# Hybrid decoder layer, one core: an opening on raw x with two gate tiles, and a merge with its gate halves in place

## The chip, the cores and the metric

The kernel runs on one NeuronCore of a Trainium2 chip. The metric is device time in microseconds (us); before the change the median of three runs is 1577.41 us (1577.34 to 1582.8). The engines are PE (TensorE: products), DVE (VectorE), ACT (ScalarE), POOL (GpSimd) and SP (which only issues DMAs). Each takes its instructions in order; they wait for one another by semaphores.

## The reference, cut to what matters

One decoder layer, sequence 1024, width 1024, all float32, x transposed to (channel, time) by the host.

```python
h = rms_norm(x, norm_mix_pre)
proj = h @ w_in        # [RWKV r,k,v, decay, rate, gate downs | S5 input u | two gates of 1024]
gates = sigmoid(proj[..., N_RWKV_COLS + S5_WIDTH:] + b_gate)
o_rwkv = rwkv7_branch(p_rwkv, ...) @ w_branch_rwkv       # a delta-rule state over time, 8 heads
o_s5   = s5_branch(u_s5, ...) @ w_branch_s5              # scan, GELU, sigmoid GLU
mixed  = (g_rwkv * o_rwkv + g_s5 * o_s5) @ w_out
x = x + rms_norm(mixed, norm_mix_post)
f = conv_ffn(rms_norm(x, norm_ffn_pre), ...)             # gated, width-3 convolution
x = x + rms_norm(f, norm_ffn_post)
```

The norm is `x * rsqrt(mean(x*x)) * g`: one factor per time step and one per channel. The factor per time step commutes with a product over channels.

## The kernel before, in words

Each float32 product is three products of halves: both operands are split into a high part (rounded, by ACT) and the rest (by DVE), and PE sums high*high, high*rest and rest*high (L174, L175, L176). One k-step is such a triple for 128 channels; a tile of output is 128 x 512 over eight k-steps. Time is cut into two halves of 512. Weights come by `load_w` (L156 to L158): the DMA on SP's queue, the high part on ACT, the rest on DVE, in rings of four split tiles (`NWH`, `NWL`) and two raw ones (`NWF`).

Stages of the front half:

- `start` (the opening): loads half 0 of x, sums its squares (`norm`: squares on ACT, pairs added on DVE, `sumsq` on PE), forms the factor per time step (`rstd`, twelve small DVE instructions), spreads it over the partitions on PE (`spread`, L284), scales x by it and by the gain (L974) and splits the result (L239, L240). Then come the S5 input tiles, two abreast (`s5_in`, 16 steps of a triple): tiles 2 and 3, then 0 and 1 of half 0, then 0 and 1 of half 1. An exit copies the psum with time reversed in eights (L1075) and stores it to `US`. `s5_setup` forms some 130 small constants on DVE.
- the S5 stage: two lanes, tables and batches, over four groups of channels. Beside them runs a list of fill: the remaining S5 inputs, `mix_in` (the RWKV inputs with their low-rank tiles), sixteen gate tiles.
- the RWKV stage: four chains (two groups of heads, two halves). Each has a front (two lanes, `rwkv_front`, with masked products L718 and L720), an inverse (62 small DVE steps between DMAs over POOL's queue), `rwkv_level`, `rwkv_chain` (eight steps of three hand-overs between PE and DVE or ACT) and `rwkv_out` (layer norm). Fill: what is left of `mix_in`, the gate tiles, and from the third chain on `merge` of half 0, `out_glu` and `merge_s5` of half 1.

The order on PE is written out by a planner (`drive`): it keeps a clock and a credit, runs a step of a lane where its due time has come, and otherwise a step of fill; while fill is left, a lane's step needs credit, which fill earns. Due times are the constants `T_...`: `T_TAB0` is the allowance between the first tables and their transposes (L556). When `merge_s5` is reached before the last chain has ended, `pause` halts the fill. The order on the other engines follows priorities (`HPN`, `HPW`, `HP2`, `HP`).

In the merge, `gate` (L1164 to L1171) loads half a gate tile into a tile `t`, forms a product of four k-steps and puts `(t + 1) * product` out; `t` is one of three `ev` buffers for half 0. The S5 outputs stand in `YU` with time split as eight by 128 and are read by halves (`s5_y`, L1142); the RWKV outputs go to `YR` (L934) and are read again by `merge_values` (L1184).

Of the kernel before, what the change touches and what calls it, by code (L numbers as in the profile page):

```python
# [31 lines left out]
VEC = {}  # L32
# [40 lines left out]
class Kern:  # L73
# [71 lines left out]
    def load_w(self, *srcs):  # L145
# [3 lines left out]
        with self.tc.high_priority(HPW):  # L149
            for src in srcs:  # L150
                for o in range(0, src.shape[1], 512):
# [5 lines left out]
                    nc.scalar.copy(h[:, :n], f[:, :n])  # L157
# [80 lines left out]
    def split(self, hi, lo, x, eng=None):  # L238
        self.nc.scalar.copy(hi, x)  # L239
        (eng or self.nc.vector).tensor_tensor(lo, x, hi.bitcast(F32), ALU.subtract)  # L240
# [47 lines left out]
    def setup(self):  # L288
# [4 lines left out]
        nc.gpsimd.dma_start(self.vecs, self.a["vec"])  # L293
# [6 lines left out]

        o, n = VEC["mu"]
        self.mu1 = self.const.tile([128, n], F32, name="mu1")
        nc.vector.tensor_scalar(self.mu1, self.vecs[:, o:o + n], -1.0, 1.0, ALU.mult, ALU.add)
        self.hb = {}
        for name in ("b_gate", "w0", "a0", "b_glu"):
            o, n = VEC[name]
            t = self.const.tile([128, n], F32, name="hb_" + name)
            nc.vector.tensor_scalar(t, self.vecs[:, o:o + n], 0.5, None, ALU.mult)
            self.hb[name] = t
# [3 lines left out]
        nc.vector.tensor_scalar(self.ka_h, self.vecs[:, o:o + n], 0.5, None, ALU.mult)  # L313
        nc.vector.tensor_scalar(self.ka_1, self.vecs[:, o:o + n], -0.5, 1.0, ALU.mult, ALU.add)


    def s5_setup(self):
# [4 lines left out]
        with self.tc.tile_pool(reuse_waits="tile", name="s5tmp", bufs=1) as pool:  # L322
# [6 lines left out]

            def ts(x, s1, s2, o0, o1=None, out=None, n=32):  # L330
                y = out if out is not None else sm(n)
                if o1 is None:
                    V.tensor_scalar(y, x, s1, None, o0)
                else:
                    V.tensor_scalar(y, x, s1, s2, o0, o1)
                return y

            def tt(x, y, op, n=32):
                z = sm(n)
                V.tensor_tensor(z, x, y, op)  # L340
                return z

            def stt(x, sc, y, o0, o1):
                z = sm()
                V.scalar_tensor_tensor(z, x, sc, y, o0, o1)
# [28 lines left out]
            xr = tt(lr, dt, ALU.mult)  # L374
            th = tt(li, dt, ALU.mult)
            s1, s2, q = exp_parts(xr)
            s12 = tt(s1, s2, ALU.mult)
            em1 = tt(s12, q, ALU.mult)
            sm1 = ts(s12, -1.0, None, ALU.add)
            em1 = tt(em1, sm1, ALU.add)  # L380
            r = ts(em1, 1.0, None, ALU.add)

# [14 lines left out]
            def sincos(x):  # L397
                x = ts(x, -PI_, PI_, ALU.max, ALU.min)
                si, co, ab = sm(), sm(), sm()
                nc.scalar.activation(si, x, AF.Sin)  # L400
                nc.scalar.activation(ab, x, AF.Abs)
# [5 lines left out]
            nc.scalar.activation(sh, xh, AF.Sin)  # L407

# [1641 lines left out]
```

## Time and profile before

| | |
|---|---|
| median of the runs | 1577.41 us |
| profiled execution | 1580.96 us, span 1578.8 us |
| mean granted clock of PE | 0.975 |
| PE busy | 1484.3 us (94%) |
| DVE busy | 1160.7 us (74%) |
| ACT busy | 727.8 us (46%) |
| POOL busy | 198.6 us (13%) |

Times in the profile count from the first instruction. A row of the timeline gives start, length, engine, line and operation, then `out<-in` by tile names and the number of instructions; in brackets stands the idle time of the engine before it and what ended it. A row of a group ends with the group's busy time, the mean ns of one, and the idle time before them. `gm`, `chk`, `rp` are psum tiles; `hh`/`hl` and `wh`/`wl` the parts of an operand and of a weight.

### The profile page before, as it was taken

The page shows a single profiled execution, that of the slowest core. Times are in us where ns is not written, and L with a number is a line of the kernel's source. Part 1 is how long each engine was busy: PE and PEld are TensorE (multiplying, and loading weights), DVE is VectorE, ACT ScalarE, POOL GpSimd, SP SyncE. Part 2 cuts the span into 40 slices and gives each one's busy share as a digit, 9 for nine tenths or more (in the row PEclk, how much of TensorE's full clock was granted, in tenths as well). Part 3 has the DMA queues.
Part 4 walks back from the last instruction along what each step waited for, and adds up shares of the span by engine and source line. Part 5 has one row for each costly group of instructions (what it writes and reads, how often), then busy time and mean ns, then how long its engine had stood idle before and what let it go on. Part 6 is the DMA issues. An engine that isn't in the chain of part 4 may idle for free.

```text
span 1578.8 us, 23472 instructions
## 1 busy us (share of the span) xinstructions
PE 1484.3 (94%) x8608; PEld 1190.0 (75%) x8608; DVE 1160.7 (74%) x2130; ACT 727.8 (46%) x1202; POOL 198.6 (13%) x342
## 2 busy tenths in 40 slices
PE   5998999999998998889999999999999999999995
PEld 4886888777676786556678788888888887888774
DVE  7888865756444578586477869788888888697767
ACT  5444443332353354347544546455555555444351
POOL 0042110123220123212020011000000000000000
PEclk9999999999997998999999999999999999999997
DMA  6354333443333275445264666233333336944612
GB/s 195 112 162 128 101 120 134 147 127 95 106 98 125 63 225 166 127 120 160 84 202 131 218 239 210 96 120 114 113 107 111 117 114 212 328 153 138 229 60 106
DMA packets 113890, 225.50 MB, mean 143 GB/s; under 512 B 22848, under 2 KB 28992, under 8 KB 113776
## 3 DMA queue, kind: packets, MB, share of 16 engines
q1 hardware_dynamic: 90432, 154.54, 30.9%
q0 software_dynamic: 21184, 65.23, 12.6%
q10 hardware_dynamic: 2160, 4.24, 0.7%
q8 instruction: 67, 1.10, 0.3%
q14 instruction: 47, 0.39, 0.1%
HBM read 163.93 MB, written 57.93 MB: 141 GB/s over the span
## 4 chain that ended last, share of the span: by engine, by line
PE 70%; DVE 10%; DMA 8%; issue 6%; ACT 3%; POOL 2%; SPq 1%; DVEq 0%; ACTq 0%; POOLq 0%
PE gm L174 9%; PE gm L175 8%; PE gm L176 8%; PE rp L1486 5%; PE rp L1488 5%; PE rp L1487 5%; DMA st<-in_w_down_dram 3%; PE mm L1487 2%; PE mm L1486 2%; PE mm L1488 2%; PE mm L175 2%; PE mm L176 2%; PE mm L174 2%; PE d L1664 2%; PE ch L174 2%
## 5 line engine op out<-in xcount | busy, mean ns | idle before, releaser
L174 PE MATMUL gm<-hh,wh 128*128 128x512 f32 x688 | 295.5, 430 | 11.6 <-DVE hl L1171 4.7
L175 PE MATMUL gm<-hl,wh 128*128 128x512 f32 x688 | 275.2, 400 | 0.7 <-DVE hl L240 0.6
L176 PE MATMUL gm<-hh,wl 128*128 128x512 f32 x688 | 275.1, 400 | 0.0
L158 DVE TENSOR_TENSOR wl<-wf,wh 128x512 fp32r<-128x512 f32 x178 | 121.6, 686 | 94.1 <-ACT wh L157 92.8
L157 ACT CAST wh<-wf 128x512 fp32r<-128x512 f32 x178 | 109.9, 620 | 143.1 <-PE gm L175 82.7
L174 PEld LDWEIGHTS gm<-hh,wh 128*128 128x128 f32 x688 | 132.1, 192 | 46.7 <-DVE hl L1171 4.8
L176 PEld LDWEIGHTS gm<-hh,wl 128*128 128x128 f32 x688 | 132.3, 192 | 29.8 <-DVE wl L158 0.7
L175 PEld LDWEIGHTS gm<-hl,wh 128*128 128x128 f32 x688 | 132.7, 193 | 25.7 <-DVE hl L240 2.9
L1664 PE MATMUL d<-xl,wh 128*128 128x512 f32 x308 | 121.0, 393 | 6.1 <-DVE xl L240 6.1
L1663 PE MATMUL d<-xh,wh 128*128 128x512 f32 x308 | 120.8, 392 | 2.0 <-DVE zg L1516 2.0
L1665 PE MATMUL d<-xh,wl 128*128 128x512 f32 x308 | 120.4, 391 | 0.0
L1486 PE MATMUL rp<-t,h 128*128 128x512 f32 x252 | 98.3, 390 | 1.4 <-ACT p L1500 1.4
L1488 PE MATMUL rp<-t,l 128*128 128x512 f32 x252 | 98.0, 389 | 0.0
L1487 PE MATMUL rp<-t,h 128*128 128x512 f32 x252 | 98.0, 389 | 0.0
L1664 PEld LDWEIGHTS d<-xl,wh 128*128 128x128 f32 x308 | 58.2, 189 | 19.7 <-DVE xl L240 7.8
L1663 PEld LDWEIGHTS d<-xh,wh 128*128 128x128 f32 x308 | 58.1, 189 | 14.9 <-DVE zg L1516 2.4
L240 DVE TENSOR_TENSOR l<-r,h 128x1024 fp32r<-128x1024 f32 (+1 forms) x40 | 38.9, 972 | 39.5 <-ACT h L239 39.4
L1665 PEld LDWEIGHTS d<-xh,wl 128*128 128x128 f32 x308 | 58.3, 189 | 11.9
L239 ACT CAST h<-r 128x1024 fp32r<-128x1024 f32 (+1 forms) x40 | 33.9, 849 | 71.0 <-PE rp L1487 67.2
L1507 DVE SCALAR_TENSOR_TENSOR y<-zv,vecs,y 128x1023 f32<-128x1023 f32 (+1 forms) x42 | 53.8, 1280 | 10.2 <-ACT y L1505 10.2
L1486 PEld LDWEIGHTS rp<-t,h 128*128 128x128 f32 x252 | 47.3, 188 | 12.0 <-ACT p L1500 2.2
L1488 PEld LDWEIGHTS rp<-t,l 128*128 128x128 f32 x252 | 47.3, 188 | 9.8
(455 smaller groups left out, 3357.7 us busy)
## 6 DMA issues: line engine op xcount, KB each, us to landing
r<-in_w_up_dram SPq DMA_DIRECT2D x42, 512.0 KB, 3.7
wf<-in_w_in_dram SPq DMA_DIRECT2D x72, 256.0 KB, 2.9
st<-in_w_down_dram SPq DMA_DIRECT2D x55, 256.0 KB, 4.4
st<-ACT SPq DMA_DIRECT2D x44, 256.0 KB, 4.5
ACT<-y POOLq DMA_DIRECT2D x21, 512.0 KB, 2.9
GT<-ev POOLq DMA_DIRECT2D x32, 256.0 KB, 3.4
wf<-in_w_br_dram SPq DMA_DIRECT2D x32, 256.0 KB, 2.9
wf<-in_w_out_dram SPq DMA_DIRECT2D x32, 256.0 KB, 2.9
```

The costliest lines, as they stand in the source:

```text
L157: nc.scalar.copy(h[:, :n], f[:, :n])
L158: nc.vector.tensor_tensor(l[:, :n], f[:, :n], h[:, :n].bitcast(F32), ALU.subtract)
L174: mm(ps, a, xh[k], start=a0, stop=False)
L175: mm(ps, a, xl[k], start=False, stop=False)
L176: mm(ps, b, xh[k], start=False, stop=z0)
L1486: mm(ps, wh[:, c], xh, start=first and k == 0, stop=False, skip_group_check=True)
L1487: mm(ps, wh[:, c], xl, start=False, stop=False, skip_group_check=True)
L1488: mm(ps, wl[:, c], xh, start=False, stop=k == 3, skip_group_check=True)
L1507: V.scalar_tensor_tensor(y[:, lag:], z[:, 0:1024 - lag], self.vec(nme, i), y[:, lag:], ALU.mult, ALU.add)
L1663: mm(ps, wh[:, c], xh[:, x], start=start, stop=False, skip_group_check=True)
L1664: mm(ps, wh[:, c], xl[:, x], start=False, stop=False, skip_group_check=True)
L1665: mm(ps, wl[:, c], xh[:, x], start=False, stop=stop, skip_group_check=True)
```

## The change

It has four parts.

1. The opening. The S5 input tiles of half 0 are made from x times the gain alone, split in high part and rest (`self.raw`, held in the slots of the second half), while the squares are still being summed. The factor per time step, copied to `rbc`, is applied at the exit, which moves from ACT to DVE. Weights are loaded by half tiles between the loads of x. The S5 constants come in two parts, ordered on DVE behind the splits, and the squares of half 1 are ordered behind the fifth split of half 0. After the S5 tiles of half 0 come gate tiles 0 and 1, abreast, for both halves (the second as the head of the fill); the S5 tiles of half 1 follow as fill. `T_TAB0` goes from 18 to 50.
2. Fronts. The two lanes take turns with their masked products (`self.masked`).
3. The merge. Gate halves are loaded into the tile that takes the result, or into the low part of the merged pair (`merged_sum`); the outputs of the second chain stay on chip (`self.kept`) instead of going through `YR`. The GLU may be opened by `merge_s5` itself. `T_LF` goes from 11.0 to 14.5.
4. `YU` is stored by halves: read rows become 2 KB long, written ones 256 bytes.

```diff
@@ norm
+        if th == 0:
+            self.raw += [self.pair(1, k) for k in range(NK)]
+        yield
         ss = self.chk()[:, 0:512]
...
+                if th == 0:
+                    hi, lo = self.raw[k + i]
+                    nc.scalar.activation(hi, x, AF.Identity, scale=g)
+                    nc.vector.scalar_tensor_tensor(lo, x, g, hi.bitcast(F32), ALU.mult, ALU.subtract)
+                op = nc.scalar.activation(sq[i], x, AF.Square)
+                if th and k == i == 0:
+                    tc.add_manual_dep(op.ins, self.splits[4][0].ins.name, ORDER)
+            op = nc.vector.tensor_tensor(sq[0], sq[0], sq[1], ALU.add)
...
+            if th and k == 0:
+                tc.add_manual_dep(op.ins, self.splits[4][1].ins.name, ORDER)
...
         self.spread(bc, y)
+        if th == 0:
+            self.rbc = pool.tile([128, 512], F32, tag="rbc", name=self.nm("rbc"))
+            nc.scalar.copy(self.rbc, bc)
+            yield
@@ s5_in
+            if raw:
+                self.nc.vector.tensor_tensor(y.rearrange("p i n -> p n i"), p[:, :, ::-1], t[:, :, ::-1], ALU.mult)
+            else:
+                self.nc.scalar.copy(y.rearrange("p i n -> p n i"), p[:, :, ::-1])
@@ start
+            half_w(0)
+            self.load_x(0, xp, xs[0], 6)
+            half_w(512)
+            self.load_x(0, xp, xs[0], 8)
...
+        a = self.s5_in((2, 3), 0, ws[0], True)
+        for k in range(4):
+            go(norms[0])
+            go(a, 2)
...
+        go(norms[0])
+        b = self.s5_in((0, 1), 0, ws[1], True)
...
+        go(norms[1])
...
+        go(b, 3)
+        go(norms[0])
+        with tc.high_priority(HPN - HPW):
+            go(a)
+        go(norms[0])
+        for _ in range(5):
             go(norms[1])
             go(b)
...
+        g = self.gate_tiles(0, 1, abreast=True)
+        go(g, 5)
+        go(norms[1], 2)
+        go(g, 4)
+        self.ws01 = self.s5_ws((0, 1))
+        with tc.high_priority(HPS):
+            next(consts, None)
+        self.started = g
@@ s5_batch
-        A.dma_start(ys.rearrange("j c g n -> (j c) g n"), y8)
+        for th in range(2):
+            A.dma_start(ys[th].rearrange("c g j n -> j c g n"), y8[:, :, th * 64:th * 64 + 64])
@@ rwkv_front
         for q in range(2):
+            yield 0, lambda: self.now >= self.masked
+            self.masked = self.now + 1.8 + T_GR
@@ rwkv_out
+            elif d["g"]:
+                self.kept.append(y1)
             else:
                 nc.sync.dma_start(self.YR[p][:, o], y1)
@@ merge and its helpers
+    def merged_sum(self, j, m, th, br, first, t, to):
+
+        yield from self.gate(j, m, th, br, to[1].bitcast(F32), t)
+        self.nc.vector.tensor_tensor(t, t, first, ALU.add)
+        self.split_half(*to, t)
...
-                yield from self.gate(0, i, 0, br[0:4], self.ev(), first[i])
+                yield from self.gate(0, i, 0, br[0:4], first[i], first[i])
...
-            t = self.ev()
-            yield from self.gate(1, m, 0, br[4:8], t, t)
-            nc.vector.tensor_tensor(t, t, first[m], ALU.add)
             mg.append(self.pair(1, (m + 4) % NK))
-            self.split_half(*mg[m], t)
+            yield from self.merged_sum(1, m, 0, br[4:8], first[m], self.ev(), mg[m])
@@ front_half
-                self.fill = [self.s5_rest(), self.mix_in()] + [self.gate_tiles(m) for m in range(14)] + [
+                self.fill = [self.started, self.s5_rest(), self.mix_in()] + [self.gate_tiles(m) for m in range(2, 14)] + [
                     self.gate_tiles(14, 15)]
@@ constants
-T_US, T_TAB0, T_TAB, T_TRIG, T_SCAN = 5.0, 18.0, 20.0, 12.0, 13.0
+T_US, T_TAB0, T_TAB, T_TRIG, T_SCAN = 5.0, 50.0, 20.0, 12.0, 13.0
```

More of the change, by code (lines that the diff above doesn't have):

```diff
@@ L299, in setup, with setup_vecs, behind @@
         nc.gpsimd.memset(self.hpi, math.pi / 2)
+    def setup_vecs(self):
+        def behind(op):
+            self.tc.add_manual_dep(op.ins, self.summed.ins.name, ORDER)
+        nc = self.nc
         o, n = VEC["mu"]
         self.mu1 = self.const.tile([128, n], F32, name="mu1")
-        nc.vector.tensor_scalar(self.mu1, self.vecs[:, o:o + n], -1.0, 1.0, ALU.mult, ALU.add)
+        behind(nc.vector.tensor_scalar(self.mu1, self.vecs[:, o:o + n], -1.0, 1.0, ALU.mult, ALU.add))
         self.hb = {}
@@ L328, in s5_setup, with behind @@
             nc.scalar.dma_start(li, a["s5_a"][1])
+            def behind(op):
+                if self.splits:
+                    self.tc.add_manual_dep(op.ins, self.splits[-1][1].ins.name, ORDER)
             def ts(x, s1, s2, o0, o1=None, out=None, n=32):
@@ L947, in inproj, with load_x @@
                 between()
-    def load_x(self, th, pool):
-        xs = []
-        for k in range(NK):
+    def load_x(self, th, pool, xs, n):
+        for k in range(len(xs), n):
             x = pool.tile([128, 512], F32, name=self.nm("x"), tag="x", bufs=16)
@@ L975, in norm @@
             h.append(self.hsplit(xs[k], k, self.hp[th]))
+            self.splits.append(self.split_ops)
         self.h[th] = h
@@ L1181, in merge_values @@
             return
-        for k in range(4):
-            hh, hl = self.pair(1, k)
-            self.nc.gpsimd.dma_start(hl.bitcast(F32), self.YR[k][:, 0:512])
-            self.br0.append((hh, hl))
-            self.split(hh, hl, hl.bitcast(F32))
+        for k in range(2):
+            self.br0.append(self.value(k, 0))
+        for k, y in enumerate(self.kept):
+            self.br0.append(self.pair(1, 2 + k))
+            self.split(*self.br0[-1], y)
     def merge(self, mg):
-        nc = self.nc
         s8 = (128, 8, 64)
@@ L1259, in merge_s5 @@
             first.append(self.early.tile([128, 512], F32, tag=f"ex{m}", name=self.nm("e"), bufs=1))
-            yield from self.gate(1, m, 1, self.br5, self.et(), first[m])
+            yield from self.gate(1, m, 1, self.br5, first[m], first[m])
             if m == 1:
@@ L1267, in merge_rk @@
     def merge_rk(self, first, mg):
[L1269 removed]
         for k in range(2):
[L1271 to L1274 removed]
+            self.br[k] = self.value(k, 1)
         yield 0
         for m in range(NK):
[L1277 to L1279 removed]
             mg.append(self.slots("eb", m) if m < 4 else [self.t2(F32R), self.t2(F32R)])
[L1281 removed]
+            yield from self.merged_sum(0, m, 1, self.br, first[m], self.t2(), mg[m])
         self.merged = True
```

201 lines of the change are left out of this document (115 added, 86 removed).

## The prediction

> **What bounds the kernel now.** I read the busy totals first, then the stretches of the front half, then the waits of PE.
>
> ```profile
> span 1578.8 us, 23472 instructions
> ...
> PE 1484.3 (94%) x8608; PEld 1190.0 (75%) x8608; DVE 1160.7 (74%) x2130; ACT 727.8 (46%) x1202; POOL 198.6 (13%) x342
> ```
>
> PE is busy for 94% of the span, so 94.5 us of it are left in which PE does nothing. The work on PE stays as it is (the same products, in another order), so the change is worth what it takes from these 94.5 us, less what it adds to them. The stretches say where they lie (columns: length, then PE, PEld, DVE, ACT and POOL busy).
>
> ```profile
> 0.00:27.10 27.10, 9.36 (x40) 8.84 (x40) 16.94 (x109) 14.13 (x25) 1.77 (x11) 1.00 0.78 250
> ...
> 85.00:255.00 170.00, 158.73 (x888) 136.27 (x887) 128.68 (x188) 74.68 (x103) 42.26 (x60) 0.98 0.38 117
> 255.00:600.00 345.00, 333.49 (x2459) 255.14 (x2458) 206.58 (x562) 137.16 (x293) 72.93 (x133) 0.96 0.41 128
> 600.00:820.00 220.00, 196.23 (x1707) 142.24 (x1706) 147.97 (x345) 109.31 (x243) 45.82 (x74) 0.95 0.46 136
> ```
>
> There are four places: 17.7 us before the first real product (27.1 - 9.36; even the 9.36 are only sums of squares and a spread), 11.3 us in the S5 stage (85 to 255), 11.5 us in the first part of the RWKV stage, and 23.8 us in its second part, where the merge and the last two chains run. The change touches all four. Behind 820 us it edits only where two loads of merge_rk land, and I count that as nothing, since the products of outproj stand ready to be run around them; without that cover it would be one load's landing.
>
> **The opening.** Today PE waits for the whole norm of half 0 before its first product. The timeline shows the start (columns: start, length, engine, instruction, then the idle time before it and what ended it).
>
> ```profile
> 6.27 0.63 ACT L964 ACTIVATE sq<-x 128x512 f32<-128x512 f32 x1 [0.86 <-DMA x<-in_x_dram]
> ...
> 10.20 0.92 SPq L156 DMA_DIRECT2D wf<-in_w_in_dram  x2
> ...
> 27.15 0.80 PE L174 MATMUL gm<-hh,wh 128*128 128x512 f32 x1 [1.49 <-ACT hh L239]
> ```
>
> The first tile of x is there at 6.27. The SP queue then stands until 10.20 with a weight load that needs a buffer back from DVE, and the last three tiles of x are queued behind it. The new order on that queue is two half weights, six tiles of x, two half weights, two tiles: the same loads, of which one more tile goes ahead of the waiting ones, and DVE gives the buffers back sooner, since the S5 constants no longer stand before the weight splits. After the change the high part of raw x is made on ACT (0.63) and the low part on DVE, so the first product can go at about 7 instead of 27.15. How far PE then gets is read in units, one unit being two tiles of w_in for one half: 16 steps of three products. A unit ends with its exit copy on ACT.
>
> ```profile
> 41.12 1.09 ACT L1075 COPY ev<-gm 128x512 f32<-128x512 f32 x1
> ...
> 68.26 1.11 ACT L1075 COPY ev<-gm 128x512 f32<-128x512 f32 x1
> ...
> 79.38 1.10 ACT L1075 COPY ev<-gm 128x512 f32<-128x512 f32 x1
> ```
>
> The first unit ends at 41.12, the third at 68.26, the fourth at 79.38: a unit without disturbance costs 11.1 us. Its first products run slowly, as the chain of waits shows.
>
> ```profile
> 31.28 0.43 PE gm L175
> 31.71 0.27 PE gm L176
> 31.98 0.23 PE gm L174
> ```
>
> They cost 0.43 us each until 4.6 us after 27.15, and 0.23 from then on. For the new first unit that gives 11 products at 0.43 and 37 at 0.23, 13.2 us, and some 3.8 us for the four groups of sums of squares between them, so from 7 it ends at 24. The supply does not hold it longer: ACT has two passes of 0.63 for each of eight tiles and four weight casts of about the same length, 12.6 us, so it is done at about 19. Against 41.12 that is a gain of 17 us.
>
> Part of it is given back at once. In the new order PE does three double steps of the second unit, then the spread of half 0, and then the sums of squares of half 1, which are ordered on DVE behind the fifth split of normalised half 0. The remaining five double steps of the second unit are queued behind them on PE, although their inputs have long been there. What DVE must do meanwhile:
>
> ```profile
> L974 DVE SCALAR_TENSOR_TENSOR x<-x,vecs,chk 128x512 f32<-128x512 f32 x16 | 11.3, 741 | 2.3 <-PE chk L284 2.3
> ...
> L240 DVE TENSOR_TENSOR hl<-x,hh 128x512 fp32r<-128x512 f32 x16 | 10.5, 684 | 0.4 <-ACT hh L239 0.4
> ```
>
> Five pairs of 0.74 + 0.68, overlapped by a tenth, are 6.4 us. The two new exits on DVE, for which no row exists, I price between a plain DVE pass (0.68) and the ACT copy of the same strided shape (1.10), and take the latter, since the write pattern is the same: 2.2 us. That makes a hole of about 8 us on PE, after which some 11 products run at 0.43 again (2.3 us). Net gain of the opening: 17 - 8 - 2 = **7 us**, with bounds of 17 (the hole is covered) and 4 (x comes later than I think). The two gate tiles that follow are work that PE would have had to do later anyway. The S5 constants and the vectors go behind the splits on DVE; the later tables cover them (below), and if that cover failed, PE would wait at the first transposes (L556) for as long as they are late.
>
> **The waits inside.** This view groups PE's waits from 30 to 860 us (columns: total, times, longest).
>
> ```profile
> PE chk L626 <- DVE t L620: 5.4, 2, 3.2
> PE gm L174 <- DVE hl L1171: 4.7, 1, 4.7
> PE rp L718 <- DVE gr L720: 4.1, 3, 3.0
> PE gm L174 <- ACT ev L1019: 4.0, 2, 3.0
> PE rp L924 <- DVE yn L918: 3.0, 1, 3.0
> PE chk L806 <- ACT gr L807: 2.7, 2, 1.6
> PE rp L718 <- DVE bk L698: 2.7, 1, 2.7
> PE chk L852 <- DVE S L877: 2.5, 2, 2.0
> PE gm L174 <- ACT ev L1057: 2.4, 1, 2.4
> ```
>
> S5 stage: 5.4 for the scan and 4.0 for the low-rank tiles. Both are late because DVE has a backlog of tables when PE arrives. With the first tables due after 50 us of fill instead of 18, DVE has more time. I take 6 of the 9.4, the scan's 5.4 and a little of the other (bounds 0 and 9.4).
>
> Masked products (L718): 6.8 us of waits for DVE. The new rule lets the two lanes take turns, 4.3 us apart. I take 5 (bounds 0 and 6.8).
>
> Merge: the 4.7 is PE waiting for a psum buffer while DVE waits for a gate half that found no ev buffer; the 2.4 is the ev ring too. With the halves landing in the buffers of the results, neither has to queue for ev. I take 6 (bounds 0 and 7.1). The two values kept on chip save two stores and two loads, which are hidden today. The S5 outputs are written 300 us before they are read, so their new layout is hidden as well.
>
> Layer norm of the last chain (L924): 3.0, and the planner's allowance for it rises from 11 to 14.5 us, so I take 3 (bounds 0 and 3).
>
> Together that is **20 us**, with bounds of 0 and 26.
>
> [...] The 4.0 us for the low-rank tiles begin at POOL, which rescales each of them (one view of POOL, one of DVE).
>
> ```profile
> 103.42 6.32 POOL L1021 TENSOR_SCALAR ev<-ev 128x512 f32<-128x512 f32 x1
> 110.04 0.56 POOL L1022 DMA_DIRECT2D TZ<-ev  x1 [0.30 <-POOL ev L1021]
> 110.64 0.63 POOL L1021 TENSOR_SCALAR ev<-ev 128x512 f32<-128x512 f32 x1
> ```
> ```profile
> 103.77 1.20 DVE L533 TENSOR_TENSOR t<-sml,s5ai 128x1024 f32<-128x1024 f32 x1
> ```
>
> The same instruction took 6.32 us while DVE was building tables, and 0.63 right after. [...]
>
> **What the change adds behind.** It takes fill away from the chains. The first table transposes stand here today:
>
> ```profile
> 87.05 1.04 PE L556 MATMUL chk<-csts,t 128*128 128x128 f32 x8
> ```
>
> Ahead of them lie four units (to 79.38) and 7.7 us of mix_in. After the change, by the yields in the code, six units lie ahead (two S5 pairs on raw x, two halves of the gate tiles, two S5 pairs of half 1) and, of the 50 us, 19 of mix_in. So 22 + 11 = 33 us of fill that stands beside the S5 and RWKV lanes today is used up before they begin, and the lanes start later by 33 us of PE work less what the opening gained. If the fill runs out before the last chain, PE pauses at merge_s5 and the chain runs alone. What that costs is read from a step of the last chain (start of one step, start of the next).
>
> ```profile
> 790.09 0.27 PE L852 MATMUL chk<-S,ar 64*64 64x64 f32 x2
> ...
> 796.27 0.45 PE L852 MATMUL chk<-S,ar 64*64 64x64 f32 x8
> ...
> 798.24 0.27 PE L863 MATMUL chb<-p,gr 64*64 64x64 f32 x2
> ...
> 799.54 0.45 PE L870 MATMUL chk<-UV,gr 128*64 128x64 f32 x8
> ```
>
> A step takes 6.18 us and has three hand-overs between PE and DVE, each with two k-steps of fill in it. A k-step is three products of 0.23, so 4.1 us of the 6.18 are fill and 2.1 are the chain's own. One hand-over, at 798.24, had a single k-step in it and took 1.30 without PE waiting; a hand-over without fill takes no longer than that, so a bare step is at most 3.9 us and, with nothing of DVE's delay known, at least 2.1. I take 3.5. Each step without fill then leaves 3.5 - 2.1 = 1.4 us of idle PE, and 33 us of missing fill are the fill of eight steps: 11 us. To this I add what follows at once where the fill ends early: the merge begins right behind the values of the second chain, whose layer norm, product with the gate and split nothing covers any longer, and the GLU tiles begin right behind their loads. I price each at the 3.0 that PE waits for a layer norm today (L924), 6 together. Sum: **17 us**, with bounds of 0 (all fill gone is won back by faster chains) and 38 (all 33 stay as idle, and 5 from the masked turns, which lengthen the lanes).
>
> **The sum.** -7 - 20 + 17 = -10. The profiled execution took 1580.96 us (span 1578.8 and 2.2 around it); with -10 it would take 1571. The median of the runs, 1577.41, is 3.5 lower, so the forecast is **1567 us**. What a measurement of this kernel can tell from no change is about 0.5%, 8 us.
>
> **Rivals.**
> *The fill runs out and the chain sets the end (slower).* The place is PE's pause at merge_s5 and the tail of the second chain. For it speaks that today's front half is level: in the last chain PE runs two k-steps into every hand-over up to 796, so there is little to spare, and that the last 220 us already hold 23.8 us of idle PE. Against it speaks that a bare chain is faster. It decides from the point where more than 27 us of the 33 stay as idle (-7 - 12 + 27 = +8). With 33 added and, since the stalls of the last stretch then come back in another place, 12 instead of 20 taken away: 1577.4 - 7 - 12 + 33 = 1591 us.
>
> *The gains cancel (same).* The hole behind the spread stays, the S5 stage stalls at its low-rank tiles as before, and only the merge and masked waits go: 1577.4 - 6 - 12 + 17 = 1576 us. This is also the time if the first part does not do what it says, because x and the weights still wait for each other on the SP queue as at 10.20.
>
> *The opening passes whole (faster still).* If the second unit covers the norm of half 0 so that the 8 us hole is absent, and the bare chain step is 2.8 us: 1577.4 - 17 - 20 + 12 = 1552 us.
>
> **How the numbers follow.** The forecast has a chance of 0.50 and its own range is 1556 to 1573, so 0.08 of it lies within 0.5% of no change; the whole opening has 0.08, cancelling 0.20, the fill running out 0.22. So faster by over 0.5% is 0.42 + 0.08 = 0.50, within 0.5% 0.28, slower by over 0.5% 0.22. The range goes from just below the whole opening to the price of the slower rival, 1551 to 1591, and leaves out some 0.2: what lies beyond these two prices.
>
> **What would show each step.** First real product at about 7 us; first unit's exit data complete at about 24; a hole of some 8 us before the sums of squares of half 1, with products at 0.43 behind it. The first L556 at about 110 to 116 instead of 87. No wait of L174 for L1171 or L1057; less than 2 us for L718; none over 1 us at L924. Idle PE between the end of the second chain and the merge, and a stretch of the last chain without fill between its hand-overs, some 11 us idle in all. The forecast is wrong if that stretch holds 25 us or more, if the first unit ends later than 30, or if the S5 stage has more than the 11.3 us of idle PE that it has now.

## The result and the profile after

The changed kernel takes **1618.93 us** (median of 6 runs, 1617.6 to 1625.54), the kernel before 1581.92 us on the same chip (1577.34 to 1583.17). The ratio is 1.0249, with a 95% interval of 1.0224 to 1.0274: 2.5% slower, where I had forecast 1567 us. The page of the profiled execution:

```profile
span 1617.2 us, 23532 instructions
...
PE 1494.8 (92%) x8608; PEld 1205.2 (75%) x8608; DVE 1174.6 (73%) x2146; ACT 735.2 (45%) x1215; POOL 191.1 (12%) x340
```

The span grew by 38.4 us. PE is busy for 10.5 us more with the same 8608 instructions, at a mean granted clock of 0.951 instead of 0.975, and idle for 122.4 instead of 94.5 us. The stretches of the prediction, after the change (length, then PE, PEld, DVE, ACT and POOL busy, clock, DMA share, GB/s):

```profile
0.00:27.10 27.10, 18.34 (x86) 15.09 (x87) 17.77 (x62) 17.59 (x30) 1.77 (x11) 1.00 0.81 265
27.10:85.00 57.90, 47.73 (x208) 40.30 (x207) 41.37 (x131) 22.16 (x38) 2.17 (x4) 0.82 0.28 83
85.00:255.00 170.00, 159.98 (x851) 134.94 (x850) 142.55 (x237) 78.96 (x111) 40.63 (x52) 0.98 0.46 134
255.00:600.00 345.00, 320.52 (x2438) 247.96 (x2438) 194.82 (x490) 131.12 (x277) 66.55 (x127) 0.97 0.39 123
600.00:820.00 220.00, 185.46 (x1451) 137.12 (x1448) 150.03 (x372) 105.94 (x222) 42.77 (x77) 0.86 0.43 130
820.00:1000.00 180.00, 169.33 (x962) 140.31 (x963) 125.15 (x258) 80.27 (x157) 11.27 (x21) 0.92 0.50 166
```

Two rows of the same view of the kernel before, which the prediction did not show:

```profile
27.10:85.00 57.90, 57.17 (x257) 45.74 (x257) 52.52 (x134) 26.26 (x41) 0.83 (x1) 1.00 0.41 119
...
820.00:1000.00 180.00, 177.35 (x831) 147.14 (x830) 143.21 (x259) 92.37 (x161) 13.34 (x25) 1.00 0.60 201
```

Idle PE by stretch, before and after: 17.7 and 8.8 (to 27), 0.7 and 10.2 (to 85), 11.3 and 10.0 (to 255), 11.5 and 24.5 (to 600), 23.8 and 34.5 (to 820), 2.7 and 10.7 (to 1000). Two things are to be seen. At 85 us the new opening has no lead: 86 + 208 = 294 PE instructions are done, against 40 + 257 = 297 before. And what grows is idle time far behind the opening, 31.8 us from 255 to 1000 (the stretches are cut by time, so the same one holds somewhat earlier work after the change). The milestones link the two: the first table product and the first product of the RWKV fronts, in the changed kernel:

```profile
123.50 1.04 PE L574 MATMUL chk<-csts,t 128*128 128x128 f32 x8
...
311.15 1.84 PE L699 MATMUL rp<-csts,gr 128*128 128x2 f32 x16
```

and the latter in the kernel before:

```profile
275.27 1.84 PE L680 MATMUL rp<-csts,gr 128*128 128x2 f32 x16
```

The tables begin 36.5 us later than before (87.05), the fronts 35.9 us later, the end comes 38.4 us later: in these two profiles the delay of the lanes is about that of the end. How it is paid for shows in the filling products themselves. The rows count L174 alone, one of the three products of a filling step (also of the output stage behind), in two stretches; first the kernel before:

```profile
580.00:620.00 40.00, 19.36 (x49) 9.19 (x48) 0.96 0.66 205
800.00:840.00 40.00, 20.07 (x49) 9.60 (x49) 0.96 0.61 198
```

then the changed one:

```profile
580.00:620.00 40.00, 5.11 (x12) 2.34 (x11) 0.88 0.68 209
800.00:840.00 40.00, 0.00 (x0) 0.00 (x0) 0.57 0.20 68
```

There is nothing left to fill with from 800 to 840, where the last chain runs bare and the granted clock falls to 0.57.

### The profile page after: what moved, and what is told of

Read it like the earlier page. It is cut to its first block, busy times and chain, and to the rows that moved or that the text cites. A ratio compares the mean times of both kernels' runs of the same rounds, so it can differ in the third digit from the quotient of the medians.

```text
span 1617.2 us, 23532 instructions
## 1 busy us (share of the span) xinstructions
PE 1494.8 (92%) x8608; PEld 1205.2 (75%) x8608; DVE 1174.6 (73%) x2146; ACT 735.2 (45%) x1215; POOL 191.1 (12%) x340
## 4 chain that ended last, share of the span: by engine, by line
PE 70%; DVE 13%; DMA 6%; issue 6%; ACT 3%; POOL 1%; SPq 0%; ACTq 0%; DVEq 0%; POOLq 0%
PE gm L174 9%; PE gm L175 7%; PE gm L176 7%; PE rp L1578 5%; PE rp L1580 5%; PE rp L1579 5%; PE mm L1578 2%; PE mm L1580 2%; PE mm L1579 2%; DMA st<-in_w_down_dram 2%; PE d L1756 2%; PE d L1757 2%; PE d L1755 2%; PE mm L175 2%; PE mm L174 2%
## 5 line engine op out<-in xcount | busy, mean ns | idle before, releaser
L174 PE MATMUL gm<-hh,wh 128*128 128x512 f32 x688 | 291.1, 423 | 15.8 <-ACT hh L991 7.1
L174 PEld LDWEIGHTS gm<-hh,wh 128*128 128x128 f32 x688 | 133.3, 194 | 49.2 <-ACT hh L991 7.1
L175 PEld LDWEIGHTS gm<-hl,wh 128*128 128x128 f32 x688 | 133.6, 194 | 27.7 <-DVE hl L992 2.1
L1755 PEld LDWEIGHTS d<-xh,wh 128*128 128x128 f32 x308 | 57.8, 188 | 11.9
L1599 DVE SCALAR_TENSOR_TENSOR y<-zv,vecs,y 128x1023 f32<-128x1023 f32 (+1 forms) x42 | 53.8, 1281 | 10.2 <-ACT y L1597 10.2
L1578 PEld LDWEIGHTS rp<-t,h 128*128 128x128 f32 x252 | 47.3, 188 | 11.9 <-ACT p L1592 2.2
```

Of the source, the lines that this page charges most:

```text
L174: mm(ps, a, xh[k], start=a0, stop=False)
L175: mm(ps, a, xl[k], start=False, stop=False)
L1578: mm(ps, wh[:, c], xh, start=first and k == 0, stop=False, skip_group_check=True)
L1599: V.scalar_tensor_tensor(y[:, lag:], z[:, 0:1024 - lag], self.vec(nme, i), y[:, lag:], ALU.mult, ALU.add)
L1755: mm(ps, wh[:, c], xh[:, x], start=start, stop=False, skip_group_check=True)
```

## The experiments

Each run is compared with runs of the kernel before on the same chip. Their medians are 1579.63 us for e1 to e4, 1581.72 for e5 to e8, 1581.15 for e9 to e13, 1580.31 for e14 to e17 and 1581.01 for e18 and e19. Intervals are 95% intervals of the ratio to the kernel before. Where two runs were made on different chips, I compare what each loses to the kernel before on its own chip.

**First theory (A).** The lanes set the length of the front half; the 22 us of gate products and the late due time ahead of them delay them, and the same products are missing later. Rival B: the tables are late on VectorE, since the S5 constants stand behind the splits. Rival: the merge part or the turns lose.

*e4_open: the opening part of the change alone, on the kernel before (merge part, turns and the halves of `YU` left away).*

```diff
 (kernel before, with norm, s5_in, start, s5_setup, front_half of the change)
-T_US, T_TAB0 = 5.0, 18.0
+T_US, T_TAB0 = 5.0, 50.0
```

> The kernel before with the opening part alone, with its T_TAB0 of 50; merge, turns and S5 outputs as before. Theory A: nearly the whole loss is here, 1605 to 1622 us, first table transposes at about 123. Rivals C1 and C2 (the loss is in the turns or the merge): 1575 to 1590 us.

1619.38 us, ratio 1.023 (1.0176 to 1.0284). The opening alone loses what the whole change loses (39.8 us over the kernel before, against 37.0).

*e3_merge: the merge part alone, on the kernel before (gate halves in place, outputs kept, `YU` by halves, `T_LF` 14.5).*

```diff
 (kernel before, with merge, merged_sum, open_glu, kept of the change)
-T_LF = 11.0
+T_LF = 14.5
```

> The kernel before with the merge part alone: gate halves in place, two values kept on chip, S5 outputs by halves, T_LF 14.5; no turns, opening as before. Theory A: the merge part is a small gain or nothing, 1570 to 1582 us, without the waits for L1171 (4.7) and for the ev ring (2.4). Rival C2 (the in-place merge costs): 1590 us or more.

1578.42 us, ratio 0.9997 (0.9967 to 1.0026): no change. Its waits of PE from 30 to 860 us (total, times, longest):

```profile
PE gm L174 <- ACT wh L157: 5.4, 1, 5.4
...
PE mm L174 <- DVE e L1176: 3.5, 1, 3.5
PE gm L174 <- ACT hh L244: 3.0, 1, 3.0
...
PE gm L174 <- DVE hl L1176: 0.5, 2, 0.3
```

Of the waits that I had counted as gain, the 4.7 for the gate's last instruction (L1171, here L1176) has fallen to 0.5 and the 2.4 for L1057 is gone. Others of the same size stand in their place, one of them (3.5) for the same instruction on another tile.

*e2_noturn: the change without the turns of the masked products.*

```diff
-            yield 0, lambda: self.now >= self.masked
-            self.masked = self.now + 1.8 + T_GR
```

> The changed kernel without the turns of the two front lanes at the masked products. Theory A (late lanes): 1612 to 1620 us, since the turns come after the delay is there (36.5 at the first tables, 39 at the first chain). Rival C1 (the turns lengthen each front by 4.3 us or more, four times on the path): 1600 to 1608 us. In both the waits of L739 for L741 should come back, from 3.0 to the 4.1 of the kernel before.

1620.69 us, ratio 1.0258 (1.0209 to 1.0306): the turns neither gain nor lose.

*e1_tab18: the change with the first tables due as early as before.*

```diff
-T_US, T_TAB0 = 5.0, 50.0
+T_US, T_TAB0 = 5.0, 18.0
```

> The changed kernel with one constant put back: T_TAB0 18 instead of 50, so that the first table transposes come after 18 us of fill, not 50. Theory A (the lanes start late and the fill is used up ahead of them: first L574 at 123.5 instead of 87.0, and 36 to 55 us stay between the two kernels at every later mark): the lanes come up to 32 us earlier, 1592 to 1602 us. Rival B (the tables themselves are late on DVE, which runs the S5 constants only behind the splits): PE waits at L574 for what the constant no longer covers, 1610 to 1620 us. Rival C (turns, merge or opening make the loss): no change, 1619 us.

1627.37 us, ratio 1.0294 (1.0251 to 1.0337). PE now waits for VectorE at the tables:

```profile
PE chk L574 <- DVE t L553: 11.3, 1, 11.3
PE chk L644 <- DVE t L638: 9.2, 2, 8.4
```

The time lies above every range expected. The tables start at 105, but the fronts start at 312, where they started at 311 without this edit. By the code they also need the mixing of the inputs, which stands in the list of filling products behind the gate tiles and the inputs of half 1. Putting the due time back alone does not help while these stand first.

**The place of the gate tiles.**

*e5_gates_back: the change with the gate tiles back in the list and the S5 inputs of half 1 directly behind those of half 0. The due time of the first tables was set from 50 to 30 as well, which the expectation does not say.*

```diff
-        g = self.gate_tiles(0, 1, abreast=True)
-        go(g, 5)
...
+        c = self.s5_in((0, 1), 1, ws[1])
+        go(c, 9)
...
-self.fill = [self.started, self.s5_rest(), self.mix_in()] + [self.gate_tiles(m) for m in range(2, 14)]
+self.fill = [self.s5_rest(), self.mix_in()] + [self.gate_tiles(m) for m in range(14)]
...
-T_US, T_TAB0 = 5.0, 50.0
+T_US, T_TAB0 = 5.0, 30.0
```

> Edit: the changed kernel with gate tiles 0 and 1 put back into the list of filling products (behind the mixing of the inputs), so that the S5 inputs of half 1 follow half 0 directly. Theory A (some 22 us of gate products ahead of the S5 inputs of half 1 and of the mixing start every lane later, and are missing as filling products at the end): the S5 inputs end 20 us earlier, the last S5 output and the end of the front come 15 to 25 us earlier than in the changed kernel, and the time is 1585 to 1603 us. Rival B (their place does not matter, the loss comes from the clock and from the hole of 10 us ahead of the sums of half 1): the hole stays, and the time is 1612 to 1622 us.

1609.4 us, ratio 1.0166 (1.0142 to 1.0191): 27.7 us over the kernel before instead of 37.0, so 9.3 are back, with the fronts at 298. That is less gain than theory A asked for and more than its rival allows.

*e6_back_ahead: with the second unit's steps ahead of the sums of half 1.*

```diff
-        for _ in range(5):
-            go(norms[1])
-            go(b)
+        go(b, 4)
+        go(norms[1], 5)
+        go(b)
```

> Edit: the run before, and the second unit's last splits and sums are issued ahead of the products of half 1, so that VectorE's squares are ready sooner. Theory A: the wait ahead of the sums of half 1 falls from 10 us to 4 or less, the clock is back at full sooner, and the time is 5 to 10 us under that of the run before (1575 to 1595 us). Rival B (the hole is filled by the work behind it anyway): the same as the run before within 4 us.

1608.81 us, ratio 1.017 (1.0146 to 1.0193). The wait fell from 10.2 to 4.8, the time stayed.

*e7_ahead: the same order in the changed kernel itself.*

```diff
-        for _ in range(5):
-            go(norms[1])
-            go(b)
+        go(b, 5)
+        go(norms[1], 5)
```

> Edit: the changed kernel as it is, only with the second unit's splits and squares issued ahead of where half 1's sums are waited for. It prices the hole and the slow products behind it by themselves. If the opening's delay is passed on to the lanes whole: 8 to 14 us less than the changed kernel (1605 to 1611 us). If the lanes are bound elsewhere (by the tables, by VectorE): no change (1617 to 1621 us).

1620.15 us, ratio 1.0237 (1.0216 to 1.0258): no change. The hole only shrank from 10.2 to 7.6, and the fronts start 2.4 us earlier (308.7 instead of 311.1); the run says that so little is not passed on to the end, and nothing of the rest.

*e8_gates_early: on the kernel before, the two gate tiles alone moved ahead.*

```diff
         go(c, 9)
+        go(self.gate_tiles(0, 1), 40)
...
-self.gate_tiles(m) for m in range(14)
+self.gate_tiles(m) for m in range(2, 14)
```

> Edit: the kernel before, with gate tiles 0 and 1 alone moved from the filling products to the place directly behind the S5 inputs' preparation. It prices the placement of the gate tiles by itself. Theory A (what lies ahead of the S5 and RWKV lanes delays their end, and the filling products are missed later): lanes end some 20 us later, 1590 to 1602 us. Rival C (TensorE's total work sets the end, so order does not matter): 1576 to 1584 us.

1591.06 us, ratio 1.0053 (1.0034 to 1.0072): 9 us for the place of two tiles, with not one product more. The first table products come 22 us later (109.3 instead of 87.0), the fronts 9. Theory A holds in kind; what the opening lost besides was open.

**Second theory (D): VectorE.** Rows of VectorE in the changed kernel: the last splits of half 1, the last long one of the constants (two short ones follow), the first pass for the table tile `t`.

```profile
75.65 1.28 DVE L240 TENSOR_TENSOR hl<-x,hh 128x512 fp32r<-128x512 f32 x2
...
92.58 1.03 DVE L505 TENSOR_SCALAR s5q<-s5ar 64x288 f32<-64x288 f32 x1
...
98.35 1.21 DVE L551 TENSOR_TENSOR t<-sml,s5ar 128x1024 f32<-128x1024 f32 x1
```

The last two of these in the kernel before:

```profile
46.74 1.03 DVE L487 TENSOR_SCALAR s5q<-s5ar 64x288 f32<-64x288 f32 x1
...
71.05 1.22 DVE L533 TENSOR_TENSOR t<-sml,s5ar 128x1024 f32<-128x1024 f32 x1
```

*e9_early_consts: e6 with the constants directly behind their first part, and the first tables due after 18 instead of 30.*

```diff
             self.setup_vecs()
+            next(consts, None)
...
-        with tc.high_priority(HPS):
-            next(consts, None)
...
-T_US, T_TAB0 = 5.0, 30.0
+T_US, T_TAB0 = 5.0, 18.0
```

> Edit: the run with the gate tiles back and the second unit ahead of the sums (e6, 1608.8 us), in which the second part of the S5 constants is no longer ordered behind the last split of half 1 on VectorE but follows the first part, and the first tables are due after 18 us of filling products, as in the kernel before. Theory D (VectorE is what the opening is bound by now: the raw splits took the place in which the constants were made, and all S5 tables stand behind the constants): the first table product of a lane starts 8 to 15 us earlier on VectorE (at 74 to 81 instead of 89), the end of the front half comes as much earlier, and the time is 1593 to 1602 us. Rival (the S5 inputs of half 1 come at 86 instead of 79 and hold everything by themselves): 1605 to 1612 us.

1588.96 us, ratio 1.0034 (1.0002 to 1.0067): 7.8 us over the kernel before instead of the 27.1 of e6, so 19 are back, more than expected. But two things were changed.

*e15_tab18_only: e6 with the due time alone.*

```diff
-T_US, T_TAB0 = 5.0, 30.0
+T_US, T_TAB0 = 5.0, 18.0
```

> Edit: e6 (1608.8 us), in which only the due time of the first tables goes back from 30 to 18 us of filling work; the constants stay behind the last split. Theory D: TensorE waits at the first tables instead, and the time is 1605 to 1612 us, so that the gain of e9 belongs to the constants. Rival: 1590 to 1598 us, the due time does most of it.

1592.19 us, ratio 1.0083 (1.0052 to 1.0113), 11.9 us over the kernel before. The due time gives some 15 of the 19 us, the constants some 4 (the intervals of e9 and e15 overlap). Theory D had it the other way round.

*e14_after_consts: the changed kernel with the constants early.*

```diff
             self.setup_vecs()
+            next(consts, None)
...
-        with tc.high_priority(HPS):
-            next(consts, None)
         self.started = g
```

> Edit: the changed kernel as it is, in which only the second part of the S5 constants follows the first instead of standing behind the last split of half 1. Theory D (all S5 tables wait on VectorE for the constants): the tables that wait fall away, the last S5 output comes 4 to 10 us earlier than 281, and the time is 1605 to 1614 us (not the whole 20, since the gate tiles and the 50 us of filling work stay ahead of the first tables). Rival E (in the changed kernel the 50 us cover the constants, as I forecast): 1617 to 1621 us.

1622.52 us, ratio 1.0263 (1.0224 to 1.0301): no gain. In the changed kernel the long due time does cover the constants, as the prediction said. (Of their two parts only the second is ordered behind the splits.)

*e13_late_consts: on the kernel before, only the constants late: in two parts as in the change, the second behind the last split of half 1.*

```diff
 (kernel before, with s5_setup of the change)
...
-            self.s5_setup()
+            consts = self.s5_setup()
+            next(consts)
...
         go(c, 9)
+        with tc.high_priority(HPN - 50000):
+            next(consts, None)
```

> Edit: the kernel before, in which alone the second part of the S5 constants is ordered behind the last split of half 1 on VectorE, as the change does it. It prices the place of the constants by itself. Theory D: the constants end some 15 us later, TensorE waits for the first tables, the S5 outputs and the end of the front come 8 to 20 us later, and the time is 1588 to 1602 us. Rival (the later tables cover it, as I forecast): 1577 to 1584 us.

1591.64 us, ratio 1.0078 (1.0053 to 1.0103). Without the long due time there is no cover, and PE waits at the tables:

```profile
PE chk L574 <- DVE ca L554: 5.4, 1, 5.4
PE chk L565 <- DVE t L544: 4.2, 1, 4.2
```

*e10_sums_first: e9 without the order of half 1's squares behind the fifth split.*

```diff
-                if th and k == i == 0:
-                    tc.add_manual_dep(op.ins, self.splits[4][0].ins.name, ORDER)
...
-            if th and k == 0:
-                tc.add_manual_dep(op.ins, self.splits[4][1].ins.name, ORDER)
```

> Edit: the run before, and the squares of half 1 are no longer ordered behind the fifth split of the normalised half 0, so that they can be made as soon as x of half 1 has landed. Theory D: the spread of half 1 comes at 45 to 50 instead of 59, the wait ahead of the sums goes, the clock is never halved behind it, the S5 inputs end at 72 to 78 instead of 86, and the time is 1583 to 1594 us. Rival: VectorE has no room, what half 1 gains half 0 and the tables lose, and the time is the same as that of the run before within 4 us.

1587.58 us, ratio 1.0043 (1.0017 to 1.0068): the rival's answer, the same within 4 us. The S5 inputs end at 84 instead of 88, and the fronts stay at 290.

*e12_consts_all: e10 with all constants ahead on VectorE.*

```diff
-        with tc.high_priority(HPS):
+        with tc.high_priority(HPN + 50000):
             next(consts)
...
+        with tc.high_priority(HPN + 50000):
+            next(consts, None)
```

> Edit: the run before, and all S5 constants ahead of everything else on VectorE, so that some of the raw splits of the first unit stand behind them. The first unit ends some 5 us later (28 to 31 instead of 24), the tables can start as soon as the inputs of half 1 are split. Theory D (the tables are what counts): 1575 to 1590 us, under the run before by 3 to 10. Rival (the first unit's gain is what counts): 3 to 6 us over the run before.

1588.43 us, ratio 1.0057 (1.0033 to 1.0081): no difference either.

*e16_split_pool: e10 with half 0's low parts on GpSimd.*

```diff
-            h.append(self.hsplit(xs[k], k, self.hp[th]))
+            h.append(self.hsplit(xs[k], k, self.hp[th], eng=None if th else nc.gpsimd))
```

> Edit: e10 (1587.6 us), in which the eight low parts of the normalised half 0 are made on GpSimd instead of VectorE. If VectorE's added work is what is left of the loss, 5.5 us of it go: 1581 to 1585 us. If the two engines keep one another waiting (a GpSimd pass took 6.32 us beside table building), or VectorE is not what is left: 1586 to 1600 us.

1591.05 us, ratio 1.0077 (1.0047 to 1.0107): no gain from 5.5 us less work on VectorE. The eight low parts took 1.30 us each on GpSimd instead of 0.69, so the run takes work off VectorE and makes these parts later at once.

*e17_exit_act: e10 with plain exits on ScalarE; the scaling by the norm is left out.*

```diff
-                self.nc.vector.tensor_tensor(y.rearrange("p i n -> p n i"), p[:, :, ::-1], t[:, :, ::-1], ALU.mult)
+                self.nc.scalar.copy(y.rearrange("p i n -> p n i"), p[:, :, ::-1])
```

> Edit: e10, in which the two raw units leave as plain copies on ScalarE; the scaling by the norm is left out (the S5 inputs of half 0 stay unnormalised, which changes the values and not the work behind it). It takes 4.3 us off VectorE and the wait of the exits for the norm. If VectorE's added work is what is left: 1581 to 1585 us. If not: 1586 to 1590 us.

1584.24 us, ratio 1.0027 (1.0007 to 1.0047), with the fronts at 283 instead of 290. It loses 3.9 us to the kernel before where e10 loses 6.4; the intervals overlap, so the 2.5 us are not clear of noise. If they are real, they belong to the scaled exits: their time on VectorE or their wait for the norm. Which of the two was not told apart, and e16 does not decide it either, since its splits were slower.

**Third theory (F): what moves the first front moves the end.** The due time alone, on the kernel before, to both sides.

*e18_before_tab30*

```diff
-T_US, T_TAB0 = 5.0, 18.0
+T_US, T_TAB0 = 5.0, 30.0
```

> Edit: the kernel before, first tables due after 30 us of filling work instead of 18. Theory F: the first tables and the end of the first front come some 10 to 12 us later (285 to 287 instead of 275), and the time is 1590 to 1598 us. Rival (the order of the same products does not matter, and VectorE gets time to be ready): 1574 to 1584 us.

1586.53 us, ratio 1.0036 (1.0009 to 1.0062): slower, by 5.5 instead of the 9 to 17 expected, though the first tables (99.8 instead of 87.0) and the fronts (284 instead of 275) moved as theory F said.

*e19_before_tab8*

```diff
-T_US, T_TAB0 = 5.0, 18.0
+T_US, T_TAB0 = 5.0, 8.0
```

> Edit: the kernel before, first tables due after 8 us of filling work instead of 18. Theory F: the end of the first front comes earlier by what VectorE allows (the table inputs are there at 77 to 83 today, the first table product at 87), 2 to 6 us, and the time is 1574 to 1579 us, under that of the kernel before. Rival (VectorE is level already): no change, 1578 to 1583 us, and TensorE waits at the first tables.

1585.59 us, ratio 1.0037 (1.0014 to 1.0059): no gain, and 4.6 us lost, outside both ranges. In its profile the fronts start at 278 instead of 275 (that execution took 1579.62 us, the shortest of twelve). PE stands where the tables are not ready; this stretch held 57.17 us of PE before:

```profile
27.10:85.00 57.90, 52.93 (x240) 41.85 (x241) 51.50 (x132) 23.78 (x38) 1.05 (x2) 0.96 0.34 100
```

So both sides of 18 lose in the kernel before: with 8 PE stands at tables that VectorE has not finished, and later costs too.

**All runs by their fronts.** The columns give the start of the first front's and of the last front's products (L680 in the kernel before, L699 in the changed one) in the profiled execution, the median, and what it is over the kernel before on the same chip:

| run | first front (us) | last front (us) | time (us) | over before (us) |
|---|---|---|---|---|
| before | 275 | 586 | 1581 | |
| e19, tables due after 8 | 278 | 582 | 1585.6 | 4.6 |
| e3, merge alone | 279 | 591 | 1578.4 | -1.2 |
| e17 | 283 | 594 | 1584.2 | 3.9 |
| e13, constants late | 284 | 592 | 1591.6 | 10.5 |
| e18, tables due after 30 | 284 | 595 | 1586.5 | 5.5 |
| e8, gate tiles early | 285 | 609 | 1591.1 | 9.3 |
| e9, e10 | 290 | 603 | 1589.0, 1587.6 | 7.8, 6.4 |
| e12, e15, e16 | 293 | 604 to 606 | 1588.4, 1592.2, 1591.1 | 7.3, 11.9, 10.7 |
| e5, e6 | 298, 299 | 633, 635 | 1609.4, 1608.8 | 27.7, 27.1 |
| e4, opening alone | 305 | 637 | 1619.4 | 39.8 |
| e7, change, e2, e1, e14 | 309 to 314 | 638 to 649 | 1618.9 to 1627.4 | 37.0 to 47.7 |

The time follows the first front, but not along one line, and the small losses not closely: at 283 to 285 they lie between 3.9 and 10.5 us. Up to 293 it is some 0.6 us per us, then some 15 us for the next 6. The third column shows where the bend lies: from e15 to e5 the first front moves by 6 us and the last by 27. The filling shows the bend. In e6:

```profile
580.00:620.00 40.00, 11.27 (x26) 4.99 (x25) 0.87 0.62 186
800.00:840.00 40.00, 5.22 (x11) 2.60 (x11) 0.62 0.18 59
```

and in e15:

```profile
580.00:620.00 40.00, 17.81 (x45) 8.46 (x45) 1.00 0.88 289
800.00:840.00 40.00, 10.68 (x24) 5.11 (x24) 0.74 0.20 59
```

From e15 to e6 the filling of the last chain and that around 600 both thin out. Around 600, e6 has two waits of PE ahead of its last front for which e15 has nothing over 2.4 us from 500 to 645:

```profile
596.69 1.12 PE L770 MATMUL rp<-csts,bk 128*128 128x128 f32 x4 [9.76 <-ACT bkn L771]
...
625.64 0.79 PE L174 MATMUL gm<-hh,wh 128*128 128x512 f32 x1 [8.66 <-ACT hh L239]
```

They are of the size of the jump. Why 12 us of due time bring them about stays open, as do the last 4 us between e17 and the kernel before. No run beat the kernel before clear of noise.

## Why the prediction was wrong

The sum was -7 - 20 + 17 = -10. The profile gives +38.4, and each of the three terms failed. The first rival, that the fill runs out, names what happened, at 1591 us. None of the three signs that were to show the forecast wrong came up: the first unit ended at 24.9, not behind 30, PE was idle for 10.0 us in the S5 stretch, not for more than 11.3, and for 13.5 from 800 to 840, not 25. They watched the wrong places.

**The opening (-7).** The parts of it that I read from rows came true:

```profile
7.12 0.80 PE L174 MATMUL gm<-hh,wh 128*128 128x512 f32 x1 [7.12 <-ACT hh L991]
...
24.89 0.95 PE L258 MATMUL chk<-ones,sq 128*128 128x1 f32 x8
...
41.14 1.83 PE L258 MATMUL chk<-ones,sq 128*128 128x1 f32 x8 [10.17 <-DVE sq L996]
...
54.08 1.05 PE L258 MATMUL chk<-ones,sq 128*128 128x1 f32 x8
```

The first product goes at 7.12 (about 7), the first unit is done at 24.9 (24), where the last sums of squares of half 0 follow it, and the hole lies where I put it and is 10.2 us (8). What failed is "some 11 products run at 0.43 again (2.3 us)": from 41.14 to 54.08 eighteen products and the sums between them run slowly, 12.9 us for what takes some 7 at 0.23 a product and 0.9 a group of sums, so about 6 us are lost instead of 2.3. With the longer hole and the later end of the first unit that takes up the 7. So "a gain of 17 us" is worth nothing by the time half 1 is ready: its spread goes at 64.60, before the change at 53.32. By 85 us the lead is 0 (294 instructions against 297), not 7; my bounds were -4 and -17. Of the constants I wrote that the later tables cover them; in the changed kernel that is right (e14), at the price of the later tables.

**The waits inside (-20).** The waits of PE in the changed kernel, from 30 to 860 us:

```profile
PE rp L739 <- DVE bk L728: 8.3, 2, 7.8
PE chk L873 <- ACT yn L894: 7.9, 1, 7.9
...
PE chk L644 <- DVE t L638: 4.4, 1, 4.4
...
PE rp L739 <- DVE gr L741: 3.0, 3, 1.5
...
PE gm L174 <- ACT ev L1062: 0.7, 1, 0.7
...
PE rp L945 <- DVE yn L939: 0.6, 1, 0.6
```

The S5 stage begins 36 us later now, so I measure it from its first table product to the first product of the fronts, before and after:

```profile
87.05:275.27 188.22, 174.96 (x951) 149.26 (x950) 137.85 (x203) 84.03 (x120) 43.73 (x64) 0.97 0.39 123
```
```profile
123.50:311.15 187.65, 174.78 (x949) 149.03 (x948) 135.88 (x205) 80.85 (x114) 44.27 (x66) 0.96 0.42 124
```

It is 0.6 us shorter where I took 6. The wait for the scan, which I counted on, is 4.4 instead of 5.4; that for the low-rank tiles (L1062, before L1019) has gone from 4.0 to 0.7, and others came in their place. The masked products wait 11.3 us in the two rows instead of 6.8, where I took 5 off, and the turns do nothing (e2). The merge waits named are gone, and e3, which has the layer norm's allowance too, shows that they were worth nothing. The layer norm's own wait came down from 3.0 to 0.6 at most (L945), as forecast, without a gain. The 7.9 for L894 is another wait: a copy of the second chain's result to `yn`, which stands on ACT behind the GELU passes and casts of the S5 values for the merge. The failed step is the addition itself: the waits were read rightly, some of them went, and the work behind them came no sooner. Here the lower bound, 0, was nearest to the measurement.

The rescaling passes on POOL meet table building still:

```profile
L1064 POOL TENSOR_SCALAR ev<-ev 128x512 f32<-128x512 f32 x8 | 15.0, 1881 | 30.5 <-ACT ev L1062 30.3
```

Eight passes of 1881 ns on average, 1916 before; the longest takes 5.01 us, 6.32 before. Two of them, 5.01 us from 130.20 and 4.51 us from 136.11, ran while DVE was at tables; the next took 0.63 us at 141.52, with DVE idle. Giving DVE more time first did not spread them apart. But PE no longer waits for the tiles behind them (0.7), so these passes do not explain why only 0.6 was gained.

**The fill taken away (+17).** The mechanism is the one that I described, and its size is what I got wrong, in three places. First, the delay: I let the lanes start at 110 to 116, since the opening would pay for 4 to 10 of the 33 us; they start at 123.5. Second, "a bare step is at most 3.9 us", with 3.5 taken:

```profile
813.57 0.37 PE L873 MATMUL chk<-S,ar 64*64 64x64 f32 x2 [0.56 <-DVE S L898]
...
817.72 0.37 PE L873 MATMUL chk<-S,ar 64*64 64x64 f32 x2 [0.56 <-DVE S L898]
```

It takes 4.15 us, with the clock granted at 0.50 from 810 to 840, so bare chains win back 2.0 us a step of the 6.18 and not 2.7. Third, I let the fill run out at the last chain alone; it also thins out from 580 to 620, and the last front comes 57 us later where the first comes 36 later. The idle time of PE from 255 to 1000 grew by 31.8 us against my 17, with bounds of 0 and 38, and PE's work took 10.5 us longer at the lower clock. By its number "all 33 stay as idle" was the nearest reading; that the idle time is the missing fill one for one is not shown, since the bare steps did win time back. The rival that took the 33 missed by 28 us, 19 of them because it kept the opening's -7 and 12 of the waits.

So of the 37 us lost, going back step by step, each run by what it loses to the kernel before on its chip: 9.3 with the gate tiles back and the due time at 30 (e5), 0.6 for the order of the second unit (e6), some 15 for the due time at 18 (e15), some 4 for the constants (e9), 1.4 for the sums (e10) and 2.5 for the scaled exits (e17). Differences of 4 us and less are not clear of noise, and the parts do not simply add: the two gate tiles alone cost 9.3 in the kernel before (e8), 12 us of due time 5.5 there (e18) and some 15 in e6. Some 25 of 37 are filling work used up ahead of the lanes; the raw opening itself, with the order of the fill as before, still loses 8 to 12 us (e9, e15) where I had it gain.

## What to carry to other kernels

In a kernel whose engine is kept busy by filling work beside a chain, total busy time says little: what is placed ahead of the chain's first link is paid for at its end, where the chain runs alone. Before a change of order is priced, take the first milestone that all lanes wait for (here the first front) and work out by how much it moves. Here a move of 7 to 18 us cost 4 to 12, and one of 23 us and more cost 27 to 48, so the price has to be measured, not read off one line. A wait in a profile is only a gain if the work behind it was late because of it alone; one run with that part alone (e3) settles it.

## What the runs showed of the hardware

In two stretches of the changed kernel the granted clock of PE is low although PE is counted as busy, and in both its products are small or have small ones among them:

```profile
40.00:60.00 20.00, 18.86 (x72) 16.33 (x73) 11.67 (x28) 7.29 (x14) 0.00 (x0) 0.64 0.11 32
...
800.00:840.00 40.00, 26.48 (x489) 21.89 (x484) 11.71 (x34) 17.33 (x57) 2.58 (x5) 0.57 0.20 68
```

In the first, products of 512 columns alternate with sums of one column each and follow one another without a pause from 41.1 on, the products 0.43 us apart at a granted clock of 0.50; it takes until 54.1 before the work runs fast again, with products 0.23 us apart. In the opening of the same kernel, products of 512 columns alone, started at 9.56, were fast from 13.13 on (0.23 us apart, 0.43 before), and stayed so beside later sums; the granted clock reads 1.00 there from 9.5 on. So the slow work lasted 3.6 us in the opening, with products alone, and 12.9 us behind the hole, with sums between them. Whether the sums make the difference is not shown: no run tried them by themselves.

In e16, with GpSimd and VectorE side by side, some instructions took longer and others did not. Eight splits on GpSimd took 1.30 us each, where VectorE takes 0.69 for one:

```profile
L240 POOL TENSOR_TENSOR hl<-x,hh 128x512 fp32r<-128x512 f32 x8 | 10.2, 1302 | 35.8 <-ACT hh L239 35.8
```

VectorE's sixteen passes with one operand from PSUM (`chk`) kept their length, 0.74 us on average in e10 too. But two tiny instructions that take both operands from SBUF, and take 0.16 to 0.19 us in the changed kernel, took 1.24 and 1.28 us beside GpSimd's last two splits (46.24 to 48.92):

```profile
L1012 DVE SCALAR_TENSOR_TENSOR x<-x,vecs,chk 128x512 f32<-128x512 f32 x16 | 11.1, 736 | 0.0
```
```profile
46.41 1.24 DVE L142 SCALAR_TENSOR_TENSOR rsy<-rsh,rsy 128x4 f32<-128x4 f32 x1
...
47.68 1.28 DVE L353 TENSOR_TENSOR sm<-sm,sm 128x32 f32<-128x32 f32 x1
```
